# mLSTM stage of a hybrid mLSTM and latent-attention layer: queries and keys projected one block ahead, convolutions in the second halves of the heads, two column blocks beside the last heads

## The chip, the cores and the metric

The kernel runs on one core of a Trainium2 chip. The metric is the device time of one execution in microseconds (us); a kernel's time is the median of its runs.

## What is computed

One decoder layer on 512 tokens with 2048 features. A combined projection of the normed input feeds two branches: an mLSTM with 8 heads (128 wide for queries and keys, 256 for values) behind a causal convolution of four taps and a SiLU, and latent attention (MLA). Both are gated and summed, and an output projection is added to the input. Cut to the part that matters here:

```python
proj = einsum('bsd,dn->bsn', rms_norm(x, norm_g), w_in)
(q_a, k_a, v_a, o_a, i_a, f_a, z_a, c_q, c_kv, k_r, z_b, g_a, g_b) = split(proj, ...)
qk_a = silu(causal_depthwise_conv(concatenate([q_a, k_a]), conv_w))
h_a = rms_norm(mlstm_chunkwise(q_a, k_a, v_a, i_a + ..., f_a + ...), mlstm_norm_g)
y_a = (sigmoid(o_a) * h_a * silu(z_a)) @ w_a
...                                   # latent attention gives o_b
y_b = (o_b * silu(z_b)) @ w_b
x = x + (sigmoid(g_a) * y_a + sigmoid(g_b) * y_b) @ w_out
```

## The kernel before

Every product keeps float32 accuracy: both operands are split into a high and a low part (float32r), and `mm3` (L112 to L115) issues three matmuls, high with high (L113), low with high (L114) and high with low (L115), in the order of operands of each place. `split` makes the parts: ScalarE (ACT) casts the high one (L105), VectorE (DVE) subtracts for the low one (L106). `load_w` (L134) streams weights: SyncE (SP) issues the load of a `raw` tile (4 buffers), then comes the split into `whi` (3 buffers) and `wlo` (2). A weight group serves 12 matmuls. `proj_ch` (L171) and `proj_tok` (L157) run a projection and yield after each group; after each they call `run_later` (L151), which takes one step from the list `later`.

The program is staged: projections, attention pairs, then the mLSTM heads, then the blocks of output columns (`out_b` for W_B, one for W_A, one for W_out). The heads are the stage of this case. The loop L1157 to L1182 takes the work of head after head from `heads` (L1139), and `weave` (L189) runs steps of a filler beside it: for each piece of a head (four scores, then four numerators) as many filler columns as the piece asks for (`MLSTM_STEP`, 6000). A head asks for 8 pieces, which is 16 filler steps of 3072 columns, 96 matmuls of 512 columns.

Before, the filler of heads 2p and 2p+1 is `pair_qk(p+1)` (L1098): first the block that projects the queries of the next pair, 96 matmuls, beside the even head, then the block for the keys beside the odd one. The evacuation of such a block (`conv_qk`, L969) appends for each of its two heads four steps to `later`: `first` and `second` (multiply and taps, L985 and L982, then tanh on ACT, L990), `third` (L993, then a cast on ACT, L994), `fourth` (L997). So the queries' convolution runs with the first eight weight groups of the odd head, and the keys' is run out at the pair's end, ahead of the next pair.

A head (`head_mlstm`, L1026) first broadcasts a row with a matmul (L1029), then makes four scores. For each: a maximum on DVE (L1044), exponentials on ACT (L1047), a selection on POOL (L1049), the product of `kT` and `qT`, and DVE multiplies (L1054) and splits. Tiles are `wda`, `sta` for the first two scores and `wdb`, `stb` for the last two. Then come four numerators, which ACT copies (L1066), and the normalisation's factor on DVE and POOL. `head_scale` (L1082) of head h-1 runs beside the third piece of head h, its transposes `head_out` (L1088, product L1092, copy L1094, store to `ga_d` L1095) beside the fifth. `head_load` (L1004) fetches the next head's values and gates in four loads of 512 KB.

After head 5 the pools of the projections are closed, and heads 6 and 7 have `out_b(0)` (L1129) as filler; its other operand, the attention's output, is fetched tile by tile (`reload`, L1111; `lazily`, L1120: a tile is loaded and split when a product first asks for it, and the scheduler issues its load when its buffer is free). `out_b(1)` to `out_b(3)` follow behind the heads. Tile pools and a scheduler decide the order in which each engine gets its instructions; `behind_weights` (L130) asks that an instruction be placed behind the last weight split.

## Time and profile before

| | us |
|---|---|
| median of three runs | 2159.16 |
| lowest and highest | 2156.79, 2160.86 |
| the profiled execution | 2158.7 |
| its span in the profile | 2156.8 |

In the profiled execution the heads run from about 1407 to 1664 us of the span, the last output block to its end. Engines are named PE (TensorE), DVE (VectorE), ACT (ScalarE), POOL (GpSimd) and SP (SyncE, which issues the loads). In a row of the order of time the first number is the start, the second the duration, and the bracket at the end the idle time of the engine ahead of it with what ended it. Rows that show a wait give the waiting instruction and behind the arrow the one it waited for. Ends of matmuls are modelled: a matmul of 512 columns is shown longer than the distance to the next one's start.

### The profile page before, as it was taken

How to read it: one execution, taken by the hardware profiler on the slowest of the kernel's cores; microseconds unless marked ns; L12 is line 12 of the kernel's file. 1: busy time of each engine (PE TensorE's matmuls, PEld its weight loads, DVE VectorE, ACT ScalarE, POOL GpSimd, SP SyncE). 2: the span in 40 equal slices, each digit the busy share in tenths (PEclk: the TensorE clock that was granted, in tenths of full speed). 3: DMA queues.
4: the chain of work that ended last, by engine and by line, in shares of the span. 5: the costliest groups of instructions: out<-in, count | busy, mean ns of one | idle time of the engine just before them, and what ended most of it. 6: DMA issues, size and time to landing. Idle time of an engine off the chain costs nothing.

```text
span 2156.8 us, 28863 instructions
## 1 busy us (share of the span) xinstructions
PE 2115.0 (98%) x10200; PEld 1783.3 (83%) x10200; DVE 1394.4 (65%) x2260; ACT 983.6 (46%) x2025; POOL 174.8 (8%) x306
## 2 busy tenths in 40 slices
PE   8999999999999999899999999999999999999999
PEld 8978888888888888688888888878778788888889
DVE  5877778787777778756676667766675433443333
ACT  8544444444444444445555555455564322222221
POOL 0000000000000000222222222011111000000000
PEclk9999999999999999999999999999999999999999
DMA  6645425633642562632222222464464522332433
GB/s 169 171 167 186 144 90 157 185 98 107 195 130 86 176 192 82 229 90 77 81 79 79 83 81 75 138 199 147 147 210 145 195 96 98 109 136 92 136 129 118
DMA packets 205313, 286.02 MB, mean 133 GB/s; under 512 B 31216, under 2 KB 111472, under 8 KB 204144
## 3 DMA queue, kind: packets, MB, share of 16 engines
q1 hardware_dynamic: 189040, 256.90, 39.1%
q10 hardware_dynamic: 16128, 27.27, 3.6%
q8 instruction: 80, 1.31, 0.3%
q14 instruction: 65, 0.53, 0.1%
HBM read 240.07 MB, written 44.04 MB: 132 GB/s over the span
## 4 chain that ended last, share of the span: by engine, by line
PE 53%; issue 39%; DVE 3%; ACT 2%; POOL 1%; DMA 1%; SPq 0%; ACTq 0%; DVEq 0%; POOLq 0%
PE acc L115 15%; PE acc L113 15%; PE acc L114 15%; PE aux L113 2%; PE aux L114 2%; PE aux L115 2%; DMA g<-ga 1%; PE aux L840 1%; ACT junk L236 1%; PE aux L800 1%; DVE wlo L106 0%; PE aux L816 0%; PE aux L815 0%; PE aux L786 0%; POOL rs_y L120 0%
## 5 line engine op out<-in xcount | busy, mean ns | idle before, releaser
L106 DVE TENSOR_TENSOR wlo<-raw,whi 128x512 fp32r<-128x512 f32 (+3 forms) x432 | 284.7, 661 | 403.4 <-PE acc L114 295.0
L105 ACT CAST whi<-raw 128x512 fp32r<-128x512 f32 (+3 forms) x432 | 259.1, 600 | 521.1 <-PE acc L115 370.4
L106 DVE TENSOR_TENSOR wl<-rx,wh 128x1024 fp32r<-128x1024 f32 x160 | 196.5, 1228 | 114.7 <-PE aux L512 64.7
L105 ACT CAST wh<-rx 128x1024 fp32r<-128x1024 f32 x160 | 168.9, 1055 | 177.9 <-PE acc L513 109.0
L114 PE MATMUL acc<-wlo,g 128*128 128x512 f32 x512 | 200.6, 392 | 2.4 <-DVE wlo L106 2.2
L113 PE MATMUL acc<-whi,g 128*128 128x512 f32 x512 | 200.8, 394 | 2.1 <-ACT g L105 2.1
L115 PE MATMUL acc<-whi,g 128*128 128x512 f32 x512 | 200.4, 393 | 1.2 <-DVE g L106 1.2
L105 ACT CAST wh<-rr 128x1024 fp32r<-128x1024 f32 x120 | 126.4, 1054 | 160.7 <-PE aux L513 86.5
L106 DVE TENSOR_TENSOR wl<-rr,wh 128x1024 fp32r<-128x1024 f32 x120 | 146.3, 1219 | 27.6 <-PE aux L512 14.6
L511 PE MATMUL acc<-wh,sh 128*128 128x512 f32 x400 | 155.6, 389 | 0.0
L512 PE MATMUL acc<-wl,sh 128*128 128x512 f32 x400 | 155.6, 389 | 0.0
L513 PE MATMUL acc<-wh,sl 128*128 128x512 f32 x400 | 155.6, 389 | 0.0
L114 PEld LDWEIGHTS acc<-wlo,g 128*128 128x128 f32 x512 | 96.5, 188 | 23.7 <-DVE wlo L106 4.7
L115 PEld LDWEIGHTS acc<-whi,g 128*128 128x128 f32 x512 | 96.7, 189 | 21.4 <-DVE g L106 1.6
L113 PEld LDWEIGHTS acc<-whi,g 128*128 128x128 f32 x512 | 96.2, 188 | 21.8 <-ACT g L105 2.6
L113 PE MATMUL acc<-whi,y 128*128 128x512 f32 (+1 forms) x320 | 111.1, 348 | 0.0
L115 PE MATMUL acc<-whi,y 128*128 128x512 f32 (+1 forms) x320 | 111.0, 347 | 0.0
L114 PE MATMUL acc<-wlo,y 128*128 128x512 f32 (+1 forms) x320 | 111.0, 347 | 0.0
L115 PE MATMUL acc<-h8h,wlo 128*128 128x512 f32 x256 | 100.7, 397 | 2.3 <-DVE wlo L106 2.1
L113 PE MATMUL acc<-ht,whi 128*128 128x512 f32 x256 | 101.8, 398 | 0.0
L113 PE MATMUL acc<-h8h,whi 128*128 128x512 f32 x256 | 101.7, 397 | 0.0
L114 PE MATMUL acc<-h8l,whi 128*128 128x512 f32 x256 | 100.9, 394 | 0.0
(357 smaller groups left out, 5049.0 us busy)
## 6 DMA issues: line engine op xcount, KB each, us to landing
rr<-in_w_in SPq DMA_DIRECT2D x120, 512.0 KB, 4.7
raw<-in_w_in SPq DMA_DIRECT2D x128, 256.0 KB, 2.8
rx<-in_w_in SPq DMA_DIRECT2D x40, 512.0 KB, 5.0
raw<-in_w_b SPq DMA_DIRECT2D x64, 256.0 KB, 3.1
raw<-in_w_a SPq DMA_DIRECT2D x64, 256.0 KB, 3.0
raw<-in_w_out SPq DMA_DIRECT2D x64, 256.0 KB, 3.0
raw<-in_w_ukv SPq DMA_DIRECT2D x32, 256.0 KB, 2.9
raw<-in_w_uq SPq DMA_DIRECT2D x32, 192.0 KB, 2.4
```

What stands on the lines that cost most here:

```text
L105: A.copy(dst_hi, src)
L106: return V.tensor_tensor(dst_lo, src, f32(dst_hi), ALU.subtract)
L113: PE.matmul(ps, lh, rh, start=start, stop=False)
L114: PE.matmul(ps, lh, rl, start=False, stop=False)
L115: PE.matmul(ps, ll, rh, start=False, stop=stop)
L236: A.activation(junk[:, :P], xr[:, t, :], AF.Square, accum_out=ssx[:, k, t:t + 1])
L511: PE.matmul(out[i], lh[:, tok], hi[:, n, :], start=first, stop=False, skip_group_check=cont)
L512: PE.matmul(out[i], lh[:, tok], lo[:, n, :], start=False, stop=False, skip_group_check=cont)
L513: PE.matmul(out[i], ll[:, tok], hi[:, n, :], start=False, stop=k == H8 - 1, skip_group_check=cont)
L800: PE.transpose(ps[:, t * P:(t + 1) * P], src(t), ident)
L840: PE.transpose(ps[:, j * P:(j + 1) * P], pr[:, j * P:(j + 1) * P], ident)
```

## The change

Projections of queries and keys become eight blocks, one for each head and kind (`block_qk(n)`: even n queries, odd n keys, of pair n // 2). Three of them run ahead of head 0, and head h has block h + 3 as its filler. A block's convolution is put behind eight empty entries of `later` (`CONV_WAIT`), so that it runs in the second half of the head that follows the block's; the first three blocks and the last one have none. The buffers `cv` and `th` are taken when the convolution starts. `head_scale` and `head_out` move two pieces later. After head 4 the pools change, six loads of gB are issued at once (`G_AHEAD`) and a tile is split one product ahead, and `out_b(0)` and `out_b(1)` fill heads 5, 6 and 7 and the four pieces behind head 7. In the changed file the lines of a head stand three lines lower (L1029 is L1032, L1054 is L1057, L1086 is L1089); taps, L982, are L981.

```diff
@@ -37,7 +37,7 @@
 NB_RAW, NB_W, NB_L, NB_A, NB_B, NB_HEAD, NB_T, NB_ACC, NB_AUX = 4, 3, 2, 15, 12, 17, 6, 5, 3
 NB_X, NB_RING, NB_HI, NB_LO = 5, 8, 3, 2
 
-KEYS_AHEAD, ATTN_STEP, MLSTM_STEP, OUT_AHEAD, RELOAD_STEP = 8000, 7800, 6000, 10000, 4000
+KEYS_AHEAD, ATTN_STEP, MLSTM_STEP, OUT_AHEAD, G_AHEAD, CONV_WAIT = 8000, 7800, 6000, 10000, 6, 8
 EARLY = {"lat", "c", "gz", "vh", "vl", "rope", "rk"}
 
 
@@ -966,7 +966,7 @@
     big_pool[:] = [(open_pool("bph"), NB_HEAD)]
 
 
-    def conv_qk(p, base, blk, res):
+    def conv_qk(p, base, blk, res, wait):
 
         def evac(s, ps):
             k = blk + 2 * p + s
@@ -974,28 +974,31 @@
             G.memset(xp[:, 0:3], 0.0)
             A.copy(xp[:, 3:515], ps)
             o = big([P, 2, S], F32R, "qkT")
-            cv = tmp(512, "cv")
-            th = tmp(512, "th")
+            b = []
 
             def taps(j0, j1):
                 for j in range(j0, j1):
-                    V.scalar_tensor_tensor(cv, xp[:, j:j + S], cw[:, k, j:j + 1], cv, ALU.mult, ALU.add)
+                    V.scalar_tensor_tensor(b[0], xp[:, j:j + S], cw[:, k, j:j + 1], b[0], ALU.mult, ALU.add)
 
             def first():
-                V.tensor_scalar(cv, xp[:, 3:515], cw[:, k, 3:4], None, ALU.mult)
-                taps(0, 1)
+                b.extend((tmp(512, "cv"), tmp(512, "th")))
+                with behind_weights():
+                    V.tensor_scalar(b[0], xp[:, 3:515], cw[:, k, 3:4], None, ALU.mult)
+                    taps(0, 1)
 
             def second():
                 taps(1, 3)
-                A.activation(th, cv, AF.Tanh, scale=0.5)
+                A.activation(b[1], b[0], AF.Tanh, scale=0.5)
 
             def third():
-                V.scalar_tensor_tensor(cv, th, 1.0, cv, ALU.add, ALU.mult)
-                A.copy(o[:, 0, :], cv)
+                V.scalar_tensor_tensor(b[0], b[1], 1.0, b[0], ALU.add, ALU.mult)
+                A.copy(o[:, 0, :], b[0])
 
             def fourth():
-                V.tensor_tensor(o[:, 1, :], cv, f32(o[:, 0, :]), ALU.subtract)
-
+                V.tensor_tensor(o[:, 1, :], b[0], f32(o[:, 0, :]), ALU.subtract)
+
+            if s == 0:
+                later.extend([lambda: None] * wait)
             later.extend((first, second, third, fourth))
             res.append(o)
 
@@ -1095,31 +1098,39 @@
             SP.dma_start(ga_d[h][:, s, :], go)
         hs[h] = None
 
-    def pair_qk(p):
-        qs, ks = [], []
-        yield from conv_qk(p, OFF_QA, 0, qs)
-        yield from conv_qk(p, OFF_KA, 8, ks)
+    def block_qk(n, wait=CONV_WAIT):
+
+        p, res = n // 2, []
+        yield from conv_qk(p, *((OFF_KA, 8) if n % 2 else (OFF_QA, 0)), res, wait)
         for u in range(2):
-            hs[2 * p + u].update(qT=qs[u], kT=ks[u])
+            hs[2 * p + u]["kT" if n % 2 else "qT"] = res[u]
 
     hs = [dict() for _ in range(H_A)]
-    drain(pair_qk(0))
-    while later:
-        run_later()
+    for n in range(3):
+        drain(block_qk(n, 0))
     drain(head_load(0, hs[0]))
 
     def reload(src, pool, dst):
-        for p in range(8):
-            for s in range(2):
-                g = pool.tile([P, 2, S], F32R, tag="g", name=nm("g"), bufs=16)
-                SP.dma_start(f32(g[:, 1, :]), src[p][:, s, :])
-                split(g[:, 0, :], g[:, 1, :], f32(g[:, 1, :]))
-                dst.append((g[:, 0, :], g[:, 1, :]))
-                yield RELOAD_STEP
+        g = []
+
+        def fetch():
+            p, n = divmod(len(g), 2)
+            g.append(pool.tile([P, 2, S], F32R, tag="g", name=nm("g"), bufs=16))
+            SP.dma_start(f32(g[-1][:, 1, :]), src[p][:, n, :])
+
+        for _ in range(G_AHEAD):
+            fetch()
+        yield
+        for k in range(KD):
+            if len(g) < KD:
+                fetch()
+            split(g[k][:, 0, :], g[k][:, 1, :], f32(g[k][:, 1, :]))
+            dst.append((g[k][:, 0, :], g[k][:, 1, :]))
+            yield
 
     def lazily(g, rest):
         def get(k):
-            while k >= len(g):
+            while k + 1 >= len(g) and len(g) < KD:
                 next(rest)
             return g[k]
         return get
@@ -1141,44 +1152,45 @@
             ahead = head_load(h + 1, hs[h + 1]) if h + 1 < H_A else iter(())
             for n, want in enumerate(head_mlstm(h, hs[h])):
                 next(ahead, None)
-                if h and n == 2:
+                if h and n == 4:
                     head_scale(h - 1, hs[h - 1])
-                if h and n == 4:
+                if h and n == 6:
                     head_out(h - 1, hs[h - 1])
                 yield want
             drain(ahead)
-            if h % 2:
-                yield None
-        yield OUT_AHEAD
+            yield None
+        for _ in range(2):
+            yield OUT_AHEAD
         head_scale(H_A - 1, hs[H_A - 1])
-        yield OUT_AHEAD
+        for _ in range(2):
+            yield OUT_AHEAD
         head_out(H_A - 1, hs[H_A - 1])
 
-    filler = pair_qk(1)
+    filler = block_qk(3)
     done = 0
     for want in heads():
         if want is not None:
             weave([want], filler)
             continue
         done += 1
-        if done < 4:
+        if done < 5:
             drain(filler)
-            while later:
-                run_later()
-            if done < 3:
-                filler = pair_qk(done + 1)
-            else:
-                close_pool("htp")
-                close_pool("h8p")
-                gp = open_pool("gp", "right")
-                up = open_pool("up", "right")
-                gB = []
-                get_gb = lazily(gB, reload(gb_d, gp, gB))
-                filler = out_b(0)
+            filler = block_qk(done + 3, CONV_WAIT if done < 4 else 0)
+        elif done == 5:
+            drain(filler)
+            close_pool("htp")
+            close_pool("h8p")
+            gp = open_pool("gp", "right")
+            up = open_pool("up", "right")
+            gB = []
+            rest = reload(gb_d, gp, gB)
+            next(rest)
+            get_gb = lazily(gB, rest)
+            filler = chain(out_b(0), out_b(1))
     drain(filler)
     close_pool("bph")
     g2p = open_pool("g2p")
-    for d in range(1, 4):
+    for d in range(2, 4):
         drain(out_b(d))
```

DVE, first half of head 1, before: from the second score's low part (`sta`) to the low part of the fourth weight group of that head (`wlo`).

```order
L106 TENSOR_TENSOR sta_2563_13242<-wda_2560_13239,sta_2562_13241 128x512
L1054 SCALAR_TENSOR_TENSOR wda_2560_13239<-aux_2572_13291,wda_2560_13239 128x384
L993 SCALAR_TENSOR_TENSOR cv_2548_13212<-th_2549_13213,cv_2548_13212 128x512
L1086 SCALAR_TENSOR_TENSOR og_2499_12950<-num_2528_13091,rsn_2556_13228,og_2499_12950 128x256
L106 TENSOR_TENSOR sta_2563_13242<-wda_2560_13239,sta_2562_13241 128x384
L1044 TENSOR_SCALAR wdb_2561_13240<-aux_2559_13237,ab_7349 128x128
L997 TENSOR_TENSOR qkT_2547_13211<-cv_2548_13212,qkT_2547_13211 128x512
L1086 SCALAR_TENSOR_TENSOR og_2499_12950<-num_2528_13091,rsn_2556_13228,og_2499_12950 128x256
L1054 SCALAR_TENSOR_TENSOR wdb_2561_13240<-aux_2577_13326,wdb_2561_13240 128x256
L1086 SCALAR_TENSOR_TENSOR og_2499_12950<-num_2528_13091,rsn_2556_13228,og_2499_12950 128x256 x2
L106 TENSOR_TENSOR stb_2564_13243<-wdb_2561_13240,stb_2564_13243 128x256
L106 TENSOR_TENSOR wlo_2581_13342<-raw_2579_13339,whi_2580_13341 128x512
```

The same place after.

```order
L106 TENSOR_TENSOR sta_2593_13412<-wda_2590_13409,sta_2592_13411 128x512
L106 TENSOR_TENSOR wlo_2611_13500<-raw_2609_13497,whi_2610_13499 128x512
L1057 SCALAR_TENSOR_TENSOR wda_2590_13409<-aux_2602_13456,wda_2590_13409 128x384
L1047 TENSOR_SCALAR wdb_2591_13410<-aux_2589_13407,ab_7349 128x128
L106 TENSOR_TENSOR sta_2593_13412<-wda_2590_13409,sta_2592_13411 128x384
L1047 TENSOR_SCALAR wdb_2591_13410<-aux_2589_13407,ab_7349 128x128
L106 TENSOR_TENSOR wlo_2616_13530<-raw_2614_13527,whi_2615_13529 128x512
L1057 SCALAR_TENSOR_TENSOR wdb_2591_13410<-aux_2607_13488,wdb_2591_13410 128x256
L1089 SCALAR_TENSOR_TENSOR og_2529_13104<-num_2562_13265,rsn_2586_13398,og_2529_13104 128x256 x2
L106 TENSOR_TENSOR stb_2594_13413<-wdb_2591_13410,stb_2594_13413 128x256
L1089 SCALAR_TENSOR_TENSOR og_2529_13104<-num_2562_13265,rsn_2586_13398,og_2529_13104 128x256 x2
L106 TENSOR_TENSOR wlo_2622_13560<-raw_2620_13557,whi_2621_13559 128x512
```

The steps of the convolution (L993, L997) are gone from between the scores, a weight split has moved up between them, and two scalings (L1089) stand behind the fourth score's maximum.

DVE, first half of head 0, before: between two weight splits.

```order
L106 TENSOR_TENSOR wlo_2545_13193<-raw_2543_13190,whi_2544_13192 128x512
L106 TENSOR_TENSOR sta_2504_12958<-wda_2501_12955,sta_2503_12957 128x384
L1054 SCALAR_TENSOR_TENSOR wdb_2502_12956<-aux_2518_13034,wdb_2502_12956 128x256
L1044 TENSOR_SCALAR wdb_2502_12956<-aux_2500_12953,ab_7349 128x128
L106 TENSOR_TENSOR wlo_2571_13266<-raw_2569_13263,whi_2570_13265 128x512
```

After: from the third weight split of head 0 to the fourth.

```order
L106 TENSOR_TENSOR wlo_2554_13210<-raw_2552_13207,whi_2553_13209 128x512
L994 SCALAR_TENSOR_TENSOR cv_2543_13145<-th_2544_13146,cv_2543_13145 128x512
L1057 SCALAR_TENSOR_TENSOR wda_2531_13109<-aux_2545_13163,wda_2531_13109 128x384
L1047 TENSOR_SCALAR wdb_2532_13110<-aux_2530_13107,ab_7349 128x128
L998 TENSOR_TENSOR qkT_2523_13090<-cv_2543_13145,qkT_2523_13090 128x512
L106 TENSOR_TENSOR sta_2534_13112<-wda_2531_13109,sta_2533_13111 128x384
L1057 SCALAR_TENSOR_TENSOR wdb_2532_13110<-aux_2550_13198,wdb_2532_13110 128x256
L986 TENSOR_SCALAR cv_2555_13219<-xp_2524_13091,cw_700 128x512
L1047 TENSOR_SCALAR wdb_2532_13110<-aux_2530_13107,ab_7349 128x128
L106 TENSOR_TENSOR stb_2535_13113<-wdb_2532_13110,stb_2535_13113 128x256
L981 SCALAR_TENSOR_TENSOR cv_2555_13219<-xp_2524_13091,cw_700,cv_2555_13219 128x512
L106 TENSOR_TENSOR wlo_2561_13247<-raw_2559_13244,whi_2560_13246 128x512
```

Steps of the convolution of pair 1's queries (L994, L998, L986, L981; `cv`, `qkT`) have come between the scores of head 0.

PE at the change of pools, before: the broadcast of head 6 (L1029) and the first products of `out_b(0)` with the reloaded tile `g`.

```order
L1029 MATMUL aux_2874_14861<-nT_7342,pick_7344 128x512
L113 MATMUL acc_2882_14887<-whi_2887_14893,g_2889_14897 128x512
L114 MATMUL acc_2882_14887<-wlo_2888_14894,g_2889_14897 128x512
L113 MATMUL acc_2883_14888<-whi_2887_14893,g_2889_14897 128x512
L114 MATMUL acc_2883_14888<-wlo_2888_14894,g_2889_14897 128x512
L113 MATMUL acc_2884_14889<-whi_2887_14893,g_2889_14897 128x512
L114 MATMUL acc_2884_14889<-wlo_2888_14894,g_2889_14897 128x512
L115 MATMUL acc_2882_14887<-whi_2887_14893,g_2889_14897 128x512
L115 MATMUL acc_2883_14888<-whi_2887_14893,g_2889_14897 128x512
L115 MATMUL acc_2884_14889<-whi_2887_14893,g_2889_14897 128x512
```

After: the same place, now at head 5.

```order
L1032 MATMUL aux_2847_14707<-nT_7342,pick_7344 128x512
L113 MATMUL aux_2853_14720<-qkT_2646_13709,qkT_2709_14029 128x512
L114 MATMUL aux_2853_14720<-qkT_2646_13709,qkT_2709_14029 128x512
L115 MATMUL aux_2853_14720<-qkT_2646_13709,qkT_2709_14029 128x512
L113 MATMUL aux_2866_14772<-qkT_2646_13709,qkT_2709_14029 128x384
L114 MATMUL aux_2866_14772<-qkT_2646_13709,qkT_2709_14029 128x384
L115 MATMUL aux_2866_14772<-qkT_2646_13709,qkT_2709_14029 128x384
L113 MATMUL acc_2855_14733<-whi_2860_14739,g_2841_14695 128x512
L114 MATMUL acc_2855_14733<-wlo_2861_14740,g_2841_14695 128x512
L113 MATMUL acc_2856_14734<-whi_2860_14739,g_2841_14695 128x512
L114 MATMUL acc_2856_14734<-wlo_2861_14740,g_2841_14695 128x512
L115 MATMUL acc_2855_14733<-whi_2860_14739,g_2841_14695 128x512
```

The first two scores of the head (`qkT` with `qkT`) have come ahead of the first product with `g`.

SP at the change of pools, before: loads of weights (`raw`), of head outputs to memory (`ga`) and of the reloaded tiles (`g`).

```order
L142 DMA raw_2898_14967<-in_w_b 128x512
L142 DMA raw_2904_15001<-in_w_b 128x512
L142 DMA raw_2915_15047<-in_w_b 128x512
L1115 DMA g_2889_14897<-gb0_7326 128x512
L1115 DMA g_2895_14934<-gb0_7326 128x512
L1115 DMA g_2901_14973<-gb1_7327 128x512
L1115 DMA g_2907_15007<-gb1_7327 128x512
L1115 DMA g_2918_15053<-gb2_7328 128x512
L142 DMA raw_2920_15078<-in_w_b 128x512
```

After.

```order
L142 DMA raw_2887_14891<-in_w_b 128x512
L1119 DMA g_2841_14695<-gb0_7326 128x512
L1119 DMA g_2842_14697<-gb0_7326 128x512
L1119 DMA g_2843_14699<-gb1_7327 128x512
L1119 DMA g_2844_14701<-gb1_7327 128x512
L1119 DMA g_2845_14703<-gb2_7328 128x512
L1119 DMA g_2846_14705<-gb2_7328 128x512
L1012 DMA vh_2854_14727<-vh3_1566 128x4x256
L1119 DMA g_2862_14743<-gb3_7329 128x512
L1119 DMA g_2863_14747<-gb3_7329 128x512
L1016 DMA vl_2867_14779<-vl3_1567 128x4x256
L1119 DMA g_2871_14788<-gb4_7330 128x512
```

Six loads of `g` stand behind one weight instead of five, and the loads of the next head's values (`vh`, `vl`) have come between the later ones, ahead of the next weight.

## Rows read from the trace of the kernel before

**Rows 1.** The page: an engine's busy time, share and instructions; the chain's shares.

```profile
PE 2115.0 (98%) x10200; PEld 1783.3 (83%) x10200; DVE 1394.4 (65%) x2260; ACT 983.6 (46%) x2025; POOL 174.8 (8%) x306
...
PE 53%; issue 39%; DVE 3%; ACT 2%; POOL 1%; DMA 1%; SPq 0%; ACTq 0%; DVEq 0%; POOLq 0%
```

**Rows 2.** Busy time by window: length, engines (instructions), PE's clock, DMA share, GB/s.

```profile
1436.00:1456.00 20.00, 16.68 (x73) 13.54 (x73) 17.20 (x36) 10.48 (x25) 4.33 (x15) 0.91 0.53 159
...
1508.00:1513.00 5.00, 3.73 (x20) 2.90 (x19) 4.81 (x12) 2.41 (x7) 0.51 (x1) 1.00 0.88 285
...
1592.00:1605.00 13.00, 9.66 (x31) 7.28 (x30) 11.34 (x20) 8.28 (x15) 2.79 (x6) 0.74 0.76 266
...
1407.00:1664.00 257.00, 244.27 (x1200) 201.62 (x1199) 172.82 (x354) 139.97 (x348) 38.57 (x116) 0.98 0.54 168
```

**Rows 3.** Waits of PE from 1300 to 1720: us in total, times, longest us.

```profile
PE aux L113 <- DVE wdb L1054: 4.1, 3, 2.2
...
PE acc L114 <- DVE wlo L106: 2.2, 3, 1.0
PE acc L113 <- ACT g L105: 2.1, 1, 2.1
PE acc L115 <- DVE wlo L106: 1.8, 3, 1.1
PE aux L1092 <- DVE og L1086: 1.8, 1, 1.8
PE aux L113 <- ACT qkT L994: 1.5, 2, 0.8
PE acc L115 <- DVE g L106: 1.2, 1, 1.2
```

**Rows 4.** Order of time, PE: regular matmuls, then those at the low clock.

```profile
1417.72 0.39 PE L113 MATMUL acc<-h8h,whi 128*128 128x512 f32 x1
...
1422.93 0.39 PE L115 MATMUL acc<-ht,wlo 128*128 128x512 f32 x1
...
1450.39 0.63 PE L113 MATMUL acc<-h8h,whi 128*128 128x512 f32 x1
1450.82 0.63 PE L114 MATMUL acc<-h8l,whi 128*128 128x512 f32 x1
```

**Rows 5.** Order of time, DVE, head 1: two successive weight splits.

```profile
1438.36 0.68 DVE L106 TENSOR_TENSOR wlo<-raw,whi 128x512 fp32r<-128x512 f32 x1
...
1448.22 0.68 DVE L106 TENSOR_TENSOR wlo<-raw,whi 128x512 fp32r<-128x512 f32 x1
```

**Rows 6.** DVE by line and form, 1400 to 1680: count, busy us, mean ns, idle before.

```profile
L106 DVE TENSOR_TENSOR wlo<-raw,whi 128x512 fp32r<-128x512 f32 x74 | 50.9, 688 | 61.9 <-PE acc L115 32.0 <-PE acc L114 16.5 <-issue 7.5
L982 DVE SCALAR_TENSOR_TENSOR cv<-xp,cw,cv 128x512 f32<-128x512 f32 x42 | 31.3, 746 | 0.1
L1086 DVE SCALAR_TENSOR_TENSOR og<-num,rsn,og 128x256 f32<-128x256 f32 x32 | 14.9, 482 | 5.6 <-POOL rsn L1079 5.6
...
L997 DVE TENSOR_TENSOR qkT<-cv,qkT 128x512 fp32r<-128x512 f32 x14 | 9.6, 683 | 1.0 <-ACT qkT L994 0.9
L985 DVE TENSOR_SCALAR cv<-xp,cw 128x512 f32<-128x512 f32 x14 | 6.8, 483 | 7.0 <-ACT xp L975 7.0
...
L1044 DVE TENSOR_SCALAR wdb<-aux,ab 128x128 f32<-128x128 f32 x16 | 5.5, 341 | 0.0
L1054 DVE SCALAR_TENSOR_TENSOR wda<-aux,wda 128x384 f32<-128x384 f32 x8 | 4.4, 552 | 0.7 <-POOL wda L1049 0.7
...
L1054 DVE SCALAR_TENSOR_TENSOR wdb<-aux,wdb 128x256 f32<-128x256 f32 x8 | 3.4, 421 | 1.2 <-POOL wdb L1049 1.2
```

**Rows 7.** Order of time, ACT: the first casts of reloaded tiles.

```profile
1594.56 1.31 ACT L105 CAST g<-g 128x512 fp32r<-128x512 f32 x2 [0.75 <-DMA g<-gb]
```

**Rows 8.** DMA issues from 1585 to 1606: count, KB each, median us to landing.

```profile
g<-gb SPq DMA_DIRECT2D x13, 256.0 KB, 5.3
```

**Rows 9.** Line L1029 on PE: the first matmul of each head, first and last start.

```profile
L1029 PE MATMUL aux<-nT,pick x8: 393/393/397, 1407.8 to 1628.1; 128*128 128x512 f32 x8
```

## The prediction

> **What bounds the kernel now.** I read the page's busy shares first, then its chain of work, then the busy time by window in the mLSTM heads, the list of TensorE's waits there, and last the order of time at single places. TensorE (PE) is busy 98% of the span, and the chain is mostly matmuls and their issue [rows 1]. The change adds and removes no instruction, so it can gain only where PE stands still or runs at the lower clock. A good part of that lies in the heads: of the 257.0 us from 1407 to 1664, PE is busy for 244.3 and idle for 12.7, at a mean clock of 0.98 [rows 2]. A gap costs more than its length, since the pipeline fills again behind it: matmuls of 512 columns that follow each other start every 0.227 us (24 rows from 1417.72 to 1422.93) and are shown as 0.39 us long [rows 4], so I add 0.39 - 0.227 = 0.16 us for each. PE's waits in the stage are of seven kinds [rows 3].
>
> What feeds PE here is VectorE (DVE). In the first half of each odd head the four scores, the convolution of the next pair's queries and the scaling of the head before share it, in program order. In head 1 the low part of one weight group starts at 1438.36 and the next one at 1448.22 [rows 5]; taps, activation steps and scaling stand between them. So PE waits for the last score's weights (wdb, L1054) and then for that group (wlo). No engine is full over the stage: DVE works 172.8 of 257 us [rows 2]. What is wrong is the place of the work, not its amount.
>
> **What the change takes away.**
>
> (a) *First halves of heads 1, 3 and 5.* PE waits 4.1 us for wdb in three waits and 1.8 us for wlo (at L115) in three [rows 3]: six gaps, 4.1 + 1.8 + 6 x 0.16 = 6.9 us. Behind the pair in head 1 the clock falls: that window shows 0.91 [rows 2], and eight matmuls start 0.43 us apart instead of 0.227 [rows 4], 8 x 0.2 = 1.6. Together 8.5. In the new order the first half of heads 1 to 4 holds the scores, the weight splits and the scaling, and no tap ahead of the last score's product. The work goes to the second half, where PE has no score to wait for; its only customer on DVE there is wlo. Ahead of one wlo stand up to four operations of at most 0.75 us [rows 6], 3.0 us, against 12 matmuls (2.7 us) and the numerators between them. A head lasts (1628.1 - 1407.8) / 7 = 31.5 us with its waits [rows 9]; its DVE work is 172.8 / 257 of that, 21. So I cost the move at nothing; rival 2 is its price if that cover is missing.
>
> (b) *First scores of heads 2 and 4.* They wait 1.5 us in two waits for the convolution of the keys (qkT) [rows 3], with the gaps 1.8. The keys are now projected a head earlier and convolved half a head before use. All of it goes, and nothing is late behind it.
>
> (c) *After head 7.* The transposes wait 1.8 us for the scaled output (og) [rows 3], with the gap 1.95. Now 108 matmuls of the second column block, 24.5 us, stand ahead of them. It goes.
>
> (a) to (c): 8.5 + 1.8 + 1.95 = 12.2 us.
>
> **What it adds.**
>
> (d) *Head 0.* The queries of pair 1 are projected ahead of head 0 and their convolution has no delay, so it stands beside head 0's scores, where no tap was. Ten operations come between the third and the fourth wlo. By [rows 6] they and that wlo take 0.68 x 3 + 0.75 + 0.48 + 0.55 x 2 + 0.42 x 2 + 0.34 x 2 = 5.9 us; successive operations overlap by about 0.08 (an estimate from starts against durations), which leaves 5.1. PE has 12 matmuls and three scores' matmuls in that time, 3.1 us, and I give the third group a lead of one split, 0.7. Stall: 1.3 us. Lower end: nothing, if the lead is larger. Upper end: the pair of waits in head 1 with its clock, 2.2 + 1.1 + 0.3 + 1.6 = 5.2, less four scalings (4 x 0.48) that head 0 lacks: 3.3. I take 1.3, since the operations can be counted one by one.
>
> (e) *The reload of gB.* PE waits 2.1 us for the first tile and 1.2 for its low part [rows 3]; the window's clock is 0.74 [rows 2], and about twelve matmuls start 0.43 us apart: 2.1 + 1.2 + 0.3 + 12 x 0.2 = 6.0 us at this place. In the new order both of the head's first scores (3 x 0.227, and three of three quarters of that, 1.2 us) precede the first product with gB, and six tiles are fetched before one is split. But head 5 now carries what head 6 did, and the convolution of the last keys beside it: up to the sixth weight group DVE has 39 operations, 22.9 us by durations like those of [rows 6], 19.9 less the overlaps. PE has 60 matmuls (13.6 us) and 3.8 us of scores and numerators, 17.4. DVE is late by 2.5 us at least; it can be more where it waits for the tiles' casts on ACT (the first starts at 1594.56 [rows 7]). Lower end 2.5; upper end 8, the old 6.0 with the first wait once more. I take 4.5, about halfway to the old row: a gain of 1.5.
>
> (f) *Column block 0 to 1 inside head 7.* Four evacuations of one 512-column operation each come to DVE at once, beside that head's numerators, with no score to be late: 0.3 us, ends 0 and 1.
>
> (g) *Behind the heads* the gA tiles are fetched between weights, and PE waits 2.2 us in three waits for wlo (at L114) [rows 3], with the gaps 2.7. This order of loads stays as it was: 0, ends 2.7 gained and 1.5 lost.
>
> Sum: 12.2 - 1.3 + 1.5 - 0.3 = 12.1 us. From the profiled execution's 2158.7 that gives 2146.6; the median of the runs (2159.2) lies 0.5 above it, so 2147.
>
> **A rule that speaks against it.** The row first: the clock fell behind waits of 2.2 and 1.1 us (head 1: 0.91) and of 2.1 and 1.2 us (reload: 0.74); behind the about 0.95 and 0.35 us of head 3 it stayed at 1.00 [rows 2, 3]. The Trainium skill ("TensorE: Matmul & The Clock Gate", section "Part 1: The HAM clock gate (the "warmup" mystery)") has it that "the default state is throttled, and activity releases the throttle". By that rule a stall at head 0 could bring a spell at 1.2 GHz too; at head 1's 1.6 us the sum would be 10.5, the time 2148.5, inside the range.
>
> **The rivals.**
>
> 1. *Forecast*: 2147, own range 2142 to 2151. For it: each removed wait has a named cause, and the new order takes that cause away.
>
> 2. *The second halves collide.* The steps of a convolution go back and forth between DVE and ACT, and DVE stops in order where ACT is late, a wlo queued behind it. Against it: over the whole stage DVE waited only 1.0 us in 14 times for the cast before L997 [rows 6]. For it: ACT has numerators to copy in second halves. At 1.2 us in each of heads 1 to 4 the gain is 4.8 less: 2152.
>
> 3. *The waits move and stay.* Head 0 pays its upper end (2.0 more than taken), the reload 8 (3.5 more), and the second halves 4.8: 12.1 - 2.0 - 3.5 - 4.8 = 1.8, the time 2157.
>
> 4. *Slower: SP's queue at the reload.* SP issues in order. Twelve tiles of 256 KB, four head loads of 512 KB and a weight stand ahead of the sixth weight group, 5.3 MB. At the 266 GB/s of the old reload [rows 2] that is 20 us; from 3 us before head 5 on, it is there 17 us into the head, and needed at 17.4. For it: a tile took 5.3 us to land [rows 8], and one head load must wait for a buffer that head 5's scores still read. Against it: the 266 GB/s came with the DMA engines 76% busy [rows 2], so there is room. It decides below about 140 GB/s: the group would land at 35, 18 us late, and the time be 2147 + 18 = 2165. The Trainium skill ("DMA: Bandwidth & Descriptors", section "Queues, rings and completion order") says that each DMA engine consumes descriptors in ring order; by that rule, too, a weight lands behind the tiles issued before it.
>
> **How the numbers follow.** Chances: forecast 0.69, rival 2 0.13, rival 3 0.11, rival 4 0.07. What a measurement of this kernel can tell from no change is about 0.2%, 4.3 us. Forecast and rival 2 lie below 2159.2 - 4.3 = 2154.9: faster 0.82. Rival 3: same, 0.11. Rival 4: slower, 0.07. The range reaches down to 2140 (no stall at head 0, 1.3; the reload at its lower end, 2.0; the waits of (g) gone, 2.7; 6.0 together, and 1 for single runs) and up to 2154 (rival 2 with head 0 at its upper end). It leaves out rivals 3 and 4, 0.18.
>
> **What would show it.** In the list of waits over the heads: none for wdb, for qkT at a first score, or for og after head 7 (a, b, c); one or two for wlo in head 0, 1 to 2 us (d); at the reload a first wait of about 1 us and then waits for g and wlo, with the clock 3 to 6 us in all (e); clock 1.00 in heads 1 to 4. PE should be idle in the heads for 4 to 6 us. Wrong would be waits for wlo in second halves (rival 2), a wait that ends with a weight's landing at head 5 (rival 4), or times that move in the attention or the later output blocks, which I hold to be as before.

## Result and the profile after

The changed kernel's median is 2144.40 us (2141.43 to 2145.04, four runs) against 2158.07 before, a ratio of 0.9929 (95% interval 0.9914 to 0.9945). On another chip, in a later series, it was 2140.06 against 2157.91, 0.9918 (0.9903 to 0.9933). The forecast was 2147, range 2140 to 2154. The changed kernel's profiled execution took 2141.43.

The page of the changed kernel, first row (as in [rows 1]): PE was busy 2115.0 us and is now 2105.3, in a span shorter by 17.1.

```profile
PE 2105.3 (98%) x10200; PEld 1781.2 (83%) x10200; DVE 1398.0 (65%) x2260; ACT 982.9 (46%) x2025; POOL 172.5 (8%) x306
```

Busy time by window of the changed kernel, columns as in [rows 2]: an ordinary head, the head with the reload, the stretch behind the heads.

```profile
1459.00:1487.00 28.00, 28.00 (x146) 24.02 (x145) 21.48 (x43) 16.04 (x42) 3.67 (x15) 1.00 0.56 169
1573.00:1606.00 33.00, 29.37 (x148) 24.09 (x147) 29.93 (x59) 24.08 (x58) 5.31 (x13) 1.00 0.78 266
1690.00:1720.00 30.00, 27.51 (x118) 21.47 (x116) 15.79 (x25) 14.95 (x26) 0.00 (x0) 1.00 0.84 278
```

PE does not stand still in an ordinary head any more, and the clock is 1.00 in these three windows, where it was 0.91 in head 1 and 0.74 at the reload. The list of PE's waits over the heads and behind them (1384 to 1745), against [rows 3]:

```profile
PE acc L114 <- DVE wlo L106: 2.7, 4, 1.1
PE acc L113 <- ACT whi L105: 1.6, 1, 1.6
PE acc L113 <- ACT g L105: 1.1, 1, 1.1
PE acc L115 <- DVE g L106: 0.8, 1, 0.8
```

The waits for wdb, for wlo at L115, for qkT and for og are gone; whi is new. The four waits for wlo at L114 all lie behind the heads. The heads can be measured one by one by the broadcast that begins each (L1032, before L1029; [rows 9] has the first and the last of before). The changed kernel, order of time on PE:

```profile
1430.64 0.39 PE L1032 MATMUL aux<-nT,pick 128*128 128x512 f32 x1
...
1458.67 0.39 PE L1032 MATMUL aux<-nT,pick 128*128 128x512 f32 x1
...
1487.27 0.39 PE L1032 MATMUL aux<-nT,pick 128*128 128x512 f32 x1
...
1573.07 0.39 PE L1032 MATMUL aux<-nT,pick 128*128 128x512 f32 x1
...
1606.44 0.39 PE L1032 MATMUL aux<-nT,pick 128*128 128x512 f32 x1
...
1635.04 0.39 PE L1032 MATMUL aux<-nT,pick 128*128 128x512 f32 x1
```

From one start to the next, in us (the reload is in head 6 before, in head 5 after):

| kernel | head 0 | 1 | 2 | 3 | 4 | 5 | 6 | seven heads |
|---|---|---|---|---|---|---|---|---|
| before | 28.5 | 34.1 | 30.6 | 30.5 | 30.6 | 30.6 | 35.4 | 220.3 |
| changed | 28.0 | 28.6 | 28.6 | 28.6 | 28.6 | 33.4 | 28.6 | 204.4 |

This table is the measure used below. The same program ahead of the heads takes a different time in each execution: head 0 started at 1430.64 here and 2.2 us earlier in a later execution of the same kernel, whose whole span was 2.7 shorter. So medians of a few runs on different chips tell 2 to 4 us apart poorly, and the heads' own lengths repeat to a few tenths (the reload's head took 33.4 and 33.0). Only the last series below has the changed kernel beside the others on one chip; up to there I go by the lengths of the heads.

### The profile page after: what moved, and what is told of

It reads as the page before. It is cut to its first block, busy times and chain, and to the rows that moved or that the text cites. A ratio compares the mean times of both kernels' runs of the same rounds, so it can differ in the third digit from the quotient of the medians.

```text
span 2139.7 us, 28857 instructions
## 1 busy us (share of the span) xinstructions
PE 2105.3 (98%) x10200; PEld 1781.2 (83%) x10200; DVE 1398.0 (65%) x2260; ACT 982.9 (46%) x2025; POOL 172.5 (8%) x306
## 4 chain that ended last, share of the span: by engine, by line
PE 92%; DMA 2%; DVE 2%; ACT 2%; issue 1%; POOL 1%; SPq 0%; ACTq 0%; DVEq 0%; POOLq 0%
PE acc L114 16%; PE acc L113 16%; PE acc L115 16%; PE acc L512 8%; PE acc L513 8%; PE acc L511 7%; PE aux L512 4%; PE aux L513 4%; PE aux L511 4%; PE aux L113 2%; PE aux L115 2%; PE aux L114 2%; ACT junk L236 1%; PE aux L840 1%; PE aux L800 1%
## 5 line engine op out<-in xcount | busy, mean ns | idle before, releaser
L114 PE MATMUL acc<-wlo,g 128*128 128x512 f32 x512 | 200.1, 391 | 2.8 <-DVE wlo L106 2.7
L115 PE MATMUL acc<-whi,g 128*128 128x512 f32 x512 | 199.5, 390 | 0.8 <-DVE g L106 0.8
L114 PEld LDWEIGHTS acc<-wlo,g 128*128 128x128 f32 x512 | 96.2, 188 | 24.3 <-DVE wlo L106 5.4
L115 PEld LDWEIGHTS acc<-whi,g 128*128 128x128 f32 x512 | 96.0, 188 | 21.2 <-DVE g L106 1.2
L115 PE MATMUL acc<-whi,y 128*128 128x512 f32 (+1 forms) x320 | 111.0, 347 | 0.0
L114 PE MATMUL acc<-wlo,y 128*128 128x512 f32 (+1 forms) x320 | 111.0, 347 | 0.0
L115 PE MATMUL acc<-h8h,wlo 128*128 128x512 f32 x256 | 100.2, 392 | 0.3 <-DVE wlo L106 0.3
L114 PE MATMUL acc<-h8l,whi 128*128 128x512 f32 x256 | 100.4, 392 | 0.0
```

The source lines that it names most:

```text
L114: PE.matmul(ps, lh, rl, start=False, stop=False)
L115: PE.matmul(ps, ll, rh, start=False, stop=stop)
```

## Experiments

**What made PE wait in the first halves.** My reason was the taps beside the scores (theory 1). Theory 2 is that it takes the taps and the scaling in the same half. The changed kernel, convolutions not delayed (a projection of queries or keys takes two steps of `later` for each weight group of 12 matmuls, so eight entries are four groups, half a head):

```diff
-..., G_AHEAD, CONV_WAIT = 8000, 7800, 6000, 10000, 6, 8
+..., G_AHEAD, CONV_WAIT = 8000, 7800, 6000, 10000, 6, 0
```

> The changed kernel with the convolutions of blocks 3 to 6 not delayed: they stand in the first halves of heads 1 to 4, beside the scores, and the scaling stays two pieces later, as in the changed kernel. Theory 1 (the taps beside the scores are the cause of the waits that went away): each of the four heads gets the waits of heads 3 and 5 before, 1.7 us, so 6.8 us of them and a time of 2151, with waits for wdb and wlo in the list. Theory 2 (it takes taps and scaling in the same half): each head looks as head 0 does after the change, where the taps stand beside the scores and the only wait is 0.1 us; no such waits, and 2144 to 2145.

Median 2146.59 (2141.67 to 2150.78). Heads 1 to 4 take 29.3 us instead of 28.6: 0.7 each, not the 1.7 of theory 1, and not the 0.1 of theory 2 either. There is no wait for wdb:

```profile
PE acc L115 <- DVE wlo L106: 1.3, 4, 0.4
```

The changed kernel, scaling and transposes early:

```diff
-                if h and n == 4:
+                if h and n == 2:
                     head_scale(h - 1, hs[h - 1])
-                if h and n == 6:
+                if h and n == 4:
                     head_out(h - 1, hs[h - 1])
```

> The changed kernel with the scaling and the transposes of the last head back at the third and fifth piece; the convolutions stay in the second halves. Theory 1 and theory 2 both expect no wait for wdb or wlo in heads 1 to 4 and 2144 to 2145: scaling alone (four operations of 0.48 us) is too little. A third theory, that the scaling was the cause by itself, expects waits of 1 to 2 us in each of heads 1 to 4 and 2149 to 2152. The wait for the transposes behind head 7 does not hang on this.

Median 2142.91, heads 1 to 4 at 28.6: scaling alone costs nothing there. The reload's head is shorter, 31.8, and the stretch behind the last head's start 1.5 us longer. Both edits together:

> Both of the edits: convolutions not delayed and the scaling at the third piece, in the changed kernel. Theory 1 and theory 2 expect the waits of heads 3 and 5 before in each of heads 1 to 4, 1.7 us each, so about 2151, more where the clock falls behind one (1.6 us each). If it stays at 2144 to 2146, neither taps nor scaling in the first half was what PE waited for, and the gain came from the blocks being projected one ahead.

Median 2148.66. Heads 1 to 4 take 30.45 each, as heads 2 to 5 did before, and the old pair of waits is back in each of them:

```profile
PE aux L113 <- DVE wdb L1057: 3.6, 4, 0.9
...
PE acc L115 <- DVE wlo L106: 1.5, 4, 0.4
```

So taps alone cost 0.7 a head, scaling alone 0.0, both 1.85: more than their sum. This is theory 2, if not in its strict form. What the sum misses is where VectorE gets to the next weight split. With both, head 1 (from 1456.98), no split stands between these two, 8.4 us apart; all four scalings do:

```profile
1458.44 0.69 DVE L106 TENSOR_TENSOR wlo<-raw,whi 128x512 fp32r<-128x512 f32 x1
...
1466.87 0.68 DVE L106 TENSOR_TENSOR wlo<-raw,whi 128x512 fp32r<-128x512 f32 x1
```

With the taps alone the longest distance in the first half of head 1 (from 1460.30) is 5.5 us:

```profile
1465.57 0.69 DVE L106 TENSOR_TENSOR wlo<-raw,whi 128x512 fp32r<-128x512 f32 x1
...
1471.10 0.68 DVE L106 TENSOR_TENSOR wlo<-raw,whi 128x512 fp32r<-128x512 f32 x1
```

With the scaling alone it is 4.4, in the changed kernel 4.25, and before it was 9.9 in head 1 [rows 5] and 8.4 in head 3.

The kernel with both put back is still 9.0 us under the 2157.71 of before in its series. By the heads' lengths 3.7 of it are in head 1 (weight splits 8.4 us apart instead of 9.9, and no spell at the low clock), 2.9 at the reload, and 2.0 in the head behind the reload, which has no convolution beside it and takes 28.6 us, as against 30.6 of an ordinary head before. So the two moves into second halves are not the whole gain. The kernel before with the scaling alone moved:

```diff
-                if h and n == 2:
+                if h and n == 4:
                     head_scale(h - 1, hs[h - 1])
-                if h and n == 4:
+                if h and n == 6:
                     head_out(h - 1, hs[h - 1])
```

> The kernel before with one thing changed: scaling and transposes of the last head two pieces later. The taps of the queries stay in the first halves of heads 1, 3 and 5. Theory 1 expects the waits there to stay for the most part: 6.9 us less at most 3 x 1.9, and 2154 to 2158. Theory 2 expects them to shrink to 0.1 us a head as at head 0 after the change, the clock's fall in head 1 with them: 8.5 us less, 2150. The waits at heads 2 and 4, at the reload and behind head 7 stay in both.

Median 2148.28, a ratio to before of 0.996 (0.9951 to 0.997), 6 to 11 us less by two changed numbers. Its profile is of the slowest of its ten runs (2154.41). In it heads 1 to 5 take 30.8, 29.25, 29.4, 29.2 and 29.3 us, the reload's head 33.2, the seven heads 209.9. No wait for wdb is left in its list, and none for qkT, which I had put down to the keys being convolved late:

```profile
PE acc L114 <- DVE wlo L106: 3.3, 3, 2.2
PE acc L113 <- ACT g L105: 2.1, 1, 2.1
PE acc L115 <- DVE wlo L106: 2.0, 4, 1.1
PE aux L1092 <- DVE og L1086: 1.9, 1, 1.9
```

Theory 1 falls in its strict form. It was too much work between two weight splits (now at most 6.2 us apart in the first half of head 1 and 5.5 in head 3), and the lightest of the change's moves already takes away 8.5 of the 13.4 us that heads 1 to 5 lost. At heads 2 and 4 two scalings had stood between the keys' last steps (before, head 2: L1086 at 1475.06 and 1477.12). In this execution 4.1 us are lost again behind the heads: from the last head's start to the last stage it takes 349.9 us, before 345.8. Why is open; waits for wlo of up to 2.2 us and spells at the low clock lie there, and one profile does not tell whether the other nine runs lose it too.

**The reload in head 5.** Three waits remain: 1.1 (g), 0.8 (g's low part), 1.6 (whi). The last one ends here, in the changed kernel, on PE:

```profile
1595.29 0.97 PE L113 MATMUL acc<-whi,g 128*128 128x512 f32 x3 [1.61 <-ACT whi L105]
```

ACT had been waiting for the weight to land,

```profile
1594.62 0.62 ACT L105 CAST whi<-raw 128x512 fp32r<-128x512 f32 x1 [0.77 <-DMA raw<-in_w_b]
```

and SP had issued nothing between these two loads; behind the second stands the weight (raw):

```profile
1578.23 0.53 SPq L1119 DMA_DIRECT2D g<-gb  x1
1586.14 0.53 SPq L1022 DMA_DIRECT2D og<-zd  x1
1586.73 1.08 SPq L1119 DMA_DIRECT2D g<-gb  x2
1587.92 0.37 SPq L142 DMA_DIRECT2D raw<-in_w_b  x1
```

That is rival 4's mechanism at a tenth of its price. The load of head 6's gate (og) takes a buffer that head 5's scores still read; SP stood on it for 7.4 us. SP's own list of waits, 1570 to 1600, names a product of a score:

```profile
SPq L1022 <- PE aux L115: 7.2, 1, 7.2
```

Issued later:

```diff
         yield
+        if h == 6:
+            yield
+            yield
         og = c["og"] = big([P, T, 256], F32, "og")
```

> The changed kernel with one load moved: the fourth load of head 6's values (og) is issued two pieces of head 5 later. In the changed kernel SP stands on it from 1578.8 to 1586.1, since its buffer is read by head 5's scores, and weight group 6 is behind it. If that queue is the cause of PE's third wait at the reload (1.6 us for whi, 1.8 with the gap), this wait goes and the time falls by 1.5 to 1.8 us. If VectorE is late there anyway, a wait for wlo of about the same length takes its place and the time stays within 0.5 us.

Head 5 takes 31.5 us instead of 33.4 (33.0 in the second profile), and the wait for whi is gone; median 2139.02. The queue it is. With the last keys' convolution moved (two steps of `later` for each piece of head 5, so that the delay ends in the middle of the head):

```diff
-            filler = block_qk(done + 3, CONV_WAIT if done < 4 else 0)
+            filler = block_qk(done + 3, CONV_WAIT)
...
             weave([want], filler)
+            if done == 5:
+                run_later()
```

> The changed kernel with the convolution of the last keys delayed like the others and run in the second half of head 5, so that the reload shares VectorE with the scores alone. If VectorE's load is what PE waits for there, the second wait (0.8 us for g's low part, 1.0 with the gap) goes and the first one stays, since it waits for a cast on ACT behind the exponentials: 1 us less. If loads and casts bound it, all three waits stay and the time is the same within 0.5 us.

Median 2137.45, head 5 at 30.4: 2.5 to 2.9 less, nearly three times what I expected. Over the reload one wait is left,

```profile
PE aux L113 <- DVE wda L1057: 1.6, 1, 1.6
```

and the og load goes out 7.9 us into the head (which starts at 1571.61) instead of 13.1, as the scores are done earlier:

```profile
1579.51 0.53 SPq L1022 DMA_DIRECT2D og<-zd  x1
```

So the convolution beside the reload paid twice, on VectorE and, through the scores' buffer, in SP's queue. One tile ahead instead of six:

```diff
-..., G_AHEAD, CONV_WAIT = 8000, 7800, 6000, 10000, 6, 8
+..., G_AHEAD, CONV_WAIT = 8000, 7800, 6000, 10000, 1, 8
```

> The changed kernel with one tile fetched ahead at the reloads instead of six. If the six early loads are what shortened the first wait for gB, the first wait grows from 1.1 us towards the old 2.1, and waits for landings follow: 2 to 3 us more. If the two scores ahead of the first product and the splits' order did it, the time is the same within 1 us, since SP has the loads out early in any case.

Head 5 takes 31.4 us, 1.5 to 1.9 less than with six: SP gets the first six loads out at the same place anyway, and the wait for whi is gone, since two weight loads now go out ahead of og (at 1576.71 and 1582.99). But the stretch behind the last head's start becomes 2.1 us longer (324.3 against 322.2), with the reload of gA in it, and the median, 2140.94, is the changed kernel's on that chip (2140.06). The first two waits, 1.1 and 0.8, are the same as with six. As the six loads go out as early with either number, what early loads are worth is not tested by this.

**Behind head 7.** Without the column block's four pieces:

```diff
-        for _ in range(2):
-            yield OUT_AHEAD
         head_scale(H_A - 1, hs[H_A - 1])
-        for _ in range(2):
-            yield OUT_AHEAD
         head_out(H_A - 1, hs[H_A - 1])
```

> The changed kernel without the four pieces of the second column block between head 7 and its transposes; the rest of that block follows behind. The transposes must again wait for the scaled output: 1.8 us and the gap, about 2 us more than the changed kernel. A rival: the wait is hidden by the four evacuations and nothing changes.

The wait is back, 2.1 us, and from the last head's start to the first product of the last stage the kernel still takes 322.3 us (322.2 with the cover); the median is 2141.70. The waits for wlo shrank by as much, from 2.7 us in four to 1.0 in one, with a gap of 0.16 for each 2.2 us:

```profile
PE aux L1095 <- DVE og L1089: 2.1, 1, 2.1
...
PE acc L114 <- DVE wlo L106: 1.0, 1, 1.0
```

What is saved at the transposes is lost again right behind them: the cover by itself is worth nothing here. That place was tested with the low parts of the gA tiles put behind the weight splits (`late` is set for gA alone):

```diff
+            if late:
+                with behind_weights():
+                    split(g[k][:, 0, :], g[k][:, 1, :], f32(g[k][:, 1, :]))
...
-    get_ga = lazily(gA, reload(ga_d, g2p, gA))
+    get_ga = lazily(gA, reload(ga_d, g2p, gA, True))
```

> The changed kernel with the splits of the gA tiles put behind the weight splits of the block that uses them, so that no cast of a gA tile stands before a weight's cast on ACT while the tile is still under way. If these casts are the cause of the waits for wlo behind the heads (3.35 us with gaps), they go and the time falls by 3 us. If the weights land late because the tiles are issued between them, the waits stay, now for whi or the landing, and the time is the same. A third way: the splits come late in the block of W_A and PE waits there instead.

The stretch falls from 322.2 to 318.2 us; median 2138.80. But it was not the casts on ACT that moved, which I had meant; it was the subtractions on VectorE. In the changed kernel VectorE waits for the cast of a gA tile, with wlo behind it,

```profile
1705.11 0.69 DVE L106 TENSOR_TENSOR g<-g 128x512 fp32r<-128x512 f32 x1 [2.15 <-ACT g L105]
1705.72 0.68 DVE L106 TENSOR_TENSOR wlo<-raw,whi 128x512 fp32r<-128x512 f32 x1
```

and with the edit wlo comes every 2.72 us, which is 12 matmuls:

```profile
1699.82 0.69 DVE L106 TENSOR_TENSOR wlo<-raw,whi 128x512 fp32r<-128x512 f32 x1 [2.03 <-PE acc L114]
1702.54 0.69 DVE L106 TENSOR_TENSOR wlo<-raw,whi 128x512 fp32r<-128x512 f32 x1 [2.03 <-PE acc L114]
```

**Together, beside the changed kernel on one chip.** The changed kernel again:

> The changed kernel itself, once more, beside the three others on one chip: 2142 to 2145. Its runs differ by 3 to 4 us from each other. If that comes from the parts ahead of the heads, where the program is the same, the heads and the first block behind them should again take what they took in the first profile (PE idle 6.1 us between 1384 and 1720) whatever the whole run takes.

Median 2140.06, under the 2142 to 2145 that I expected; seven heads 204.0 us, against 204.4 in its first profile, and the stretch behind 322.2 in both. Of the 2.7 us between the spans 2.2 lie ahead of the heads. PE is idle for 5.3 us between 1384 and 1720, not 6.1.

> The changed kernel with two of the single edits together: the last keys' convolution in the second half of head 5, and the gA splits behind the weights. Each has its own place, so the sum of what each took from the waits is expected: PE idle between 1384 and 1720 from 6.1 us to about 2, of which 1.6 at the reload, and 4 to 5 us less than the changed kernel on the same chip. If the waits of the one come back through the other, the time stays at the better one's.

Median 2135.05, heads 201.4, stretch behind 318.2: the two gains add up, 2.5 and 4.0 by these lengths, 5.0 by the medians.

> The two edits with the later og load of head 6 as the third. With the scores of head 5 done earlier that load waits little, so nothing more is expected from it: the same as the two edits within 0.5 us. If SP's queue still costs something there, up to 1 us less.

Median 2134.45 (2132.93 to 2135.57), 0.9888 of before (0.9872 to 0.9905) and 5.6 us under the changed kernel: the lowest median, 0.6 us under the one without the later og load, whose heads (201.4) and stretch (318.2) are the same within 0.1. PE's list over the heads and behind them has one row:

```profile
PE aux L113 <- DVE wda L1060: 1.6, 1, 1.6
```

## Why the prediction was right, and where its sizes were off

The direction and the range were right, and the places but for head 0, where no stall came. The sum was 12.1 us; by the table it should have been 17.8. The runs show 13.7 (first chip) and 17.9 (second), with the spread ahead of the heads inside them. So that the first median lay within 3 us of the forecast is in part luck: the terms were 5.7 us too small in sum, and that chip's runs gave 4 us less than the table. The last row of the table is 345.8 - 322.2, from the last head's start to the last stage, less 96 x 0.227 for the half block that now lies in front.

| term | forecast | measured |
|---|---|---|
| (a), (b) five heads (after: 1 to 4 and 6) | 10.3 | 156.4 - 143.0 = 13.4 |
| (d) head 0 | -1.3 | 28.5 - 28.0 = +0.5 |
| (e) reload | 1.5 | 35.4 - 33.4 = 2.0 |
| (c), (f), (g) | 1.65 | 1.85 |

*(a), (b): cause half right, size 3 us too small.* Heads 1, 3 and 5 gave 9.4 for the 8.5 of (a), heads 2 and 4 gave 4.0 for the 1.8 of (b). In (a) I named the scaling beside the taps but put the fault on the taps. In (b) I blamed keys that were convolved late; with the scaling moved and the keys left where they were, no wait for qkT is left and both heads are 1.4 us shorter. The size failed by waits that are too short for the list, since the shown end of the matmul ahead covers them. Order of time on PE, before, head 2: 0.47 us lie between these two starts,

```profile
1479.05 0.40 PE L114 MATMUL acc<-h8l,whi 128*128 128x512 f32 x1
1479.52 0.73 PE L115 MATMUL acc<-h8h,wlo 128*128 128x512 f32 x2
```

and VectorE ends the wlo that the second one reads at 1478.78 + 0.68 = 1479.46:

```profile
1478.78 0.68 DVE L106 TENSOR_TENSOR wlo<-raw,whi 128x512 fp32r<-128x512 f32 x1
```

Two more in this head, of 0.04 and 0.13 us, end in the same way behind a multiply of VectorE (wda ends at 1484.62 and PE goes on at 1484.68, wdb at 1488.56 and 1488.62), and behind each the next matmul starts another 0.1 late. In the changed kernel, at the beginning of head 2, it is 0.23 from each matmul to the next:

```profile
1488.19 0.40 PE L113 MATMUL acc<-h8h,whi 128*128 128x512 f32 x1
1488.43 0.39 PE L114 MATMUL acc<-h8l,whi 128*128 128x512 f32 x1
1488.65 0.40 PE L115 MATMUL acc<-h8h,wlo 128*128 128x512 f32 x1
```

I should have taken the length of a head against the sum of its matmuls and not the waits alone. Why head 1 waited longer before than heads 3 and 5 the forecast did not ask: its weight splits stand 9.9 us apart, in head 3 8.4. Rival 2 did not come: the second halves hide the convolutions (28.6 in heads 1 to 4 with one and in head 6 without).

*(d): mis-sized by 1.8.* The operations took about what I gave: 5.5 us from the end of the third wlo (1436.27) to that of the fourth (1441.79), not 5.1. The changed kernel, DVE,

```profile
1435.59 0.68 DVE L106 TENSOR_TENSOR wlo<-raw,whi 128x512 fp32r<-128x512 f32 x1
...
1441.11 0.68 DVE L106 TENSOR_TENSOR wlo<-raw,whi 128x512 fp32r<-128x512 f32 x1
```

and the first use of each on PE:

```profile
1438.41 0.39 PE L115 MATMUL acc<-h8h,wlo 128*128 128x512 f32 x1
...
1441.85 0.50 PE L115 MATMUL acc<-h8h,wlo 128*128 128x512 f32 x1
```

So the lead was 2.1 us and not 0.7. What was left was 0.1. An order by itself tells how much work stands between two points, not how far ahead the first one is.

*(e): size right, reasons mixed.* 4.5 were left by the forecast, 33.4 - 28.6 = 4.8 by the table (4.4 in the second profile). The kernel before with the scaling late takes 33.2 at its reload too, with neither the scores nor the tiles moved ahead; so it is not shown that my two reasons made the gain. VectorE, which was to be 2.5 us late, ends only the wait of 0.8 in the list. Instead 1.4 to 1.9 was SP's queue, which I had as a rival that decides only at half the bandwidth. It needed no lack of bandwidth: I had named the load that must wait for its buffer, but priced the bytes ahead of the weight, and not the time that SP stands on that load. The weight behind it, issued at 1587.92, was there only at about 1594.6, when ACT began its cast. The Trainium skill has this in "DMA: Bandwidth & Descriptors", section "Anatomy of one DMA — SWDGE (gpsimd) path", a section on loads that GpSimd issues: a semaphore's wait is spent by the issuing sequencer before dispatch, not by the DMA engines. The trace agrees, here for SP: it issued nothing for 7.4 us, and moving the one load gave 1.4 to 1.9 back.

*(c): the wait went as forecast, but not its worth*: the kernel without the cover has the wait and the same stretch. So the 1.85 of the last row is not shown to be the cover's, and what made it stays open. *(g)* grew within its ends, from 2.2 us in three waits to 2.7 in four.

## What to carry to other kernels

When several kinds of work share an engine in order between two things that another engine needs, price them together: taps cost 0.7 us a head, scaling 0.0, and both 1.85. Before a large rearrangement, move the lightest piece alone; here two numbers gave more than half of the gain, and the rest of the rearrangement without that piece and without the later taps gave as much, so such parts do not add up. Look for waits also where a list names none: start against start, and the row that ended just before. Measure a stage by the time between two marks that repeat, and read the issuing queue for the load that it stands on, not only for the bytes ahead.

## What the hardware showed

The same wait is not always followed by a spell at the low clock. At the reload, waits of 1.1 and 0.8 us left the clock at 1.00 in the changed kernel:

```profile
1573.00:1585.00 12.00, 10.06 (x46) 7.82 (x45) 10.81 (x22) 10.55 (x26) 4.61 (x12) 1.00 0.98 333
```

and 1.1 and 0.55 us gave 0.87 in the kernel with the convolutions not delayed:

```profile
1577.00:1590.00 13.00, 11.33 (x44) 8.69 (x43) 10.17 (x20) 10.23 (x25) 4.38 (x12) 0.87 0.92 319
```

The old wait of 1.8 for og left 1.00 before:

```profile
1658.00:1675.00 17.00, 15.21 (x72) 12.33 (x71) 6.18 (x13) 5.00 (x8) 1.99 (x6) 1.00 0.64 208
```

The same wait (1.9) in the kernel before with the scaling late gave 0.89 in 1648 to 1664:

```profile
1648.00:1664.00 16.00, 14.12 (x60) 11.35 (x60) 6.42 (x14) 3.75 (x6) 1.99 (x6) 0.89 0.48 156
```

So a price for the clock belongs into the range, not into the sum. Executions of one kernel on one chip differ by 1 to 9 us, with mean clocks of 0.993 to 0.998.
